# A transformer trunk in fp32: the kernel orders the feed-forward units itself, and six of eight pairs go by seven products

## Chip, cores and metric

One core of a Trainium2 chip runs the whole program. The metric is device time in microseconds of one execution (lower is better), as the median of several runs. Matrix products run on TensorE (PE), elementwise work on VectorE (DVE) and ScalarE (ACT), a little on GpSimd (POOL), and SyncE (SP) issues the loads from device memory.

## The reference

Two layers over 256 tokens of width 2048, all in float32. Each layer is a mixer (attention, recurrence, pooling) and then a gated feed-forward part, each with a residual and a layer norm:

```python
def swiglu(x, w_gate, w_up, w_down):
    return (jax.nn.silu(x @ w_gate) * (x @ w_up)) @ w_down
...
        x = layer_norm(DN_ALPHA * x + y, ln_mix_g[layer], ln_mix_b[layer])
        f = swiglu(x, ffn_w_gate[layer], ffn_w_up[layer], ffn_w_down[layer])
        x = layer_norm(DN_ALPHA * x + f, ln_ffn_g[layer], ln_ffn_b[layer])
```

`w_gate` and `w_up` are 2048 x 5632, `w_down` is 5632 x 2048. The change touches the feed-forward part alone.

## The kernel before

**Products.** Every factor is split into a high and a low part in fp32r: ScalarE casts the high part (`whi`), VectorE subtracts it for the low part (`wlo`; both in `split`, L121 to L123). A product is three matmuls (`mm3`, L285): x low by w high, x high by w high, x high by w low. Each has 128 x 128 stationary values and 512 columns. Weights come as pieces of 128 x 1024 (`load_half`, L145) into `raw` (4 buffers) and `whi`, `wlo` (4 buffers, more where another ring of buffers is open).

**Feed-forward part** (`ffn`, L544). The hidden width is eleven chunks of 512. Chunks 0 and 1 go by `whole` (L548): sixteen pieces, gate and then up, four products of three matmuls each, 192 matmuls a chunk. Their result is gated (ScalarE silu, VectorE multiplication, L568), transposed on PE and split again ("flip"). Chunks 2 to 10 are nine units (`unit`, L448). A unit computes, for two token tiles, gate and up together as 2 x 2 blocks, over eight pairs of 128-deep slices. A pair costs eight products, or seven by a scheme with sums of x (`forms_of`, L404, made once per layer) and sums of w (`load_seven`, L428: VectorE makes `z` and `ze` from a raw tile `rs` of four blocks, and ScalarE and VectorE split them into `sh` and `sl`). `SEVEN` names the pairs that go by seven.

**A unit in time.** First half: for each pair of `SEVEN` four of its seven products, into four banks c11, c12, c22, c21. After the last one the banks are recombined (L472 to L477, one copy, four subtractions, one copy with a sign into c21). Second half: the other three products of those pairs, with a piece of `raw` and the split of `ze` (`zfh`, `zfl`), and the pairs by eight products. Into the first half are laid the eight steps of the down projection of earlier chunks (`down_steps`, L510: one piece, 12 matmuls) and the two flips of the chunk before (8 transposes). With five of eight pairs by seven products a unit has 192 - 15 = 177 matmuls of its own and 96 of the down projection, 273 in all.

**What sets the order.** PE's order in the units is that of the code (`keep_in_program_order` in `mm3`); `ORDER` and `GAPS` place pairs and down steps. For ScalarE, VectorE and SP a scheduler places each instruction by priorities (`tc.high_priority`). `rs`, `sh` and `sl` have two buffers, `z` one.

Of the kernel before, what the change touches and what calls it, by code (L numbers as in the profile page):

```python
# [72 lines left out]
SEVEN = (3, 4, 5, 6, 7)  # L73
GAPS = (1, 1, 1, 0, 2)
ORDER = (3, 0, 4, 5, 1, 6, 7, 2)
# [3 lines left out]
def trunk(ctx: ExitStack, tc: tile.TileContext, a, out):  # L79
# [62 lines left out]
    low = []  # L142
    first = [True]

    def load_half(src, between=()):  # L145
# [5 lines left out]
        with tc.high_priority(offset=400):  # L151
# [5 lines left out]
            for i in range(parts):  # L157
# [7 lines left out]
                with ExitStack() as order:  # L165
                    for ins in behind:
                        order.enter_context(tc.issue_after(ins))
                    low.append(split(hi[:, s, :], lo[:, s, :], raw[:, s, :]))
# [5 lines left out]

    later = []

    def half_done(n=1):
        for entry in list(later):
            entry[0] -= n
            if entry[0] <= 0:  # L180
                later.remove(entry)
                entry[1]()

    def mm_chunk(halves, lhs, outs, tok_major=False, after=None, before=None, seeded=False):
# [36 lines left out]
        else:  # L221
            for i, half in enumerate(halves):
                src = half[0]
                loaded.append(load_half(src, before(i) if before else ()))
                for kks in ((0,), (1,)) if before and i == 0 else ((0, 1),):
                    for tok in range(NT):
                        mms(i, tok, kks=kks)
                half_done()
# [175 lines left out]
    def forms_of(sp, xT, out, seven, tag):  # L404

        n = len(seven)
        xs = sp.tile([P, NT, 2 * n, P], F32, tag="rs", name="xs", bufs=2)
        fs = sp.tile([P, 4, n, P], F32, tag="z", name="fs", bufs=1)
        yield
        for t in range(NT):  # L410
            s = slice(2 * seven[0], 2 * seven[0] + 2 * n)
            nc.vector.tensor_tensor(xs[:, t], xT[0][t][:, s, :].bitcast(F32), xT[1][t][:, s, :].bitcast(F32), op=add)
            yield
        x11, x12, x21, x22 = (xs[:, t, e : 2 * n : 2, :] for t in range(2) for e in range(2))
        e, f, g, h = (fs[:, i] for i in range(4))
        nc.vector.tensor_tensor(e, x22, x21, op=sub)
        nc.vector.tensor_tensor(f, e, x11, op=add)
        yield
        nc.vector.tensor_tensor(g, x11, x21, op=sub)
        nc.vector.tensor_tensor(h, x12, f, op=sub)  # L420
        yield
        hi, lo = split_tile(sp, [P, 4, n, P], fs, tag)
        for i, p in enumerate(seven):
            x = lambda t, k: (xT[0][t][:, k, :], xT[1][t][:, k, :])
            e, f, g, h = (at((hi, lo), slice(None), j, i) for j in range(4))
            out[p] = {"11": x(0, 2 * p), "12": x(0, 2 * p + 1), "22": x(1, 2 * p + 1), "e": e, "f": f, "g": g, "h": h}

    def load_seven(sp, src, room):  # L428

        with tc.high_priority(offset=400):  # L430
            raw = sp.tile([P, 4, NCH], F32, tag="rs", name="rs", bufs=2)
            hi = sp.tile([P, 4, NCH], F32R, tag="sh", name="sh", bufs=2)
            lo = sp.tile([P, 4, NCH], F32R, tag="sl", name="sl", bufs=2)
            z = sp.tile([P, 3, NCH], F32, tag="z", name="z", bufs=1)
            ze = room
            last_load[0] = nc.sync.dma_start(raw, src).ins
            nc.scalar.copy(hi[:, 0], raw[:, 0])
            nc.vector.tensor_tensor(z[:, :2], raw[:, 0:3:2], raw[:, 3:4].to_broadcast([P, 2, NCH]), op=add)
            nc.vector.tensor_tensor(z[:, 2], z[:, 0], raw[:, 2], op=add)  # L439
            nc.vector.tensor_tensor(ze, z[:, 2], raw[:, 1], op=add)  # L440
            nc.vector.tensor_tensor(lo[:, 0], raw[:, 0], hi[:, 0].bitcast(F32), op=sub)
            split(hi[:, 1:], lo[:, 1:], z)
        return lambda i: (hi[:, i, :], lo[:, i, :]), ze


    BEGIN = ((0, "11", "c11"), (3, "f", "c12"), (1, "e", "c22"), (2, "g", "c21"))

    def unit(sp, w, lhs, forms, y, down, flips):  # L448


        def run(n):
            for _ in range(n):
                next(down, None)

        for _ in range(NT):
            run(1)
            flips.pop(0)()
        run(1)
        b = {n: bank("un", 4) for n in ("c11", "c12", "c22", "c21")}
        edge, room = {}, None  # L460
        for i, (p, gap) in enumerate(zip(SEVEN, GAPS)):
            if i % 2:
                room = ap_.tile([P, 4, T], F32R, tag=("y4h", "y4l")[i // 2], name="ze4", bufs=1)
                room = room.rearrange("p (e a) t -> p e (a t)", e=2).bitcast(F32)
            own = room[:, (i + 1) % 2] if i else sp.tile([P, NCH], F32, tag="ze", name="ze", bufs=1)
            wt, edge[p] = load_seven(sp, w[p], own)
            for j, x, name in BEGIN:
                mm3(b[name], forms[p][x], wt(j), i == 0, i == len(SEVEN) - 1, True)
            if i == len(SEVEN) - 1:
                with tc.high_priority(offset=1000):  # L470
# [780 lines left out]
```

## Time and profile before

| what | us |
|---|---|
| median of 3 runs | 2186.62 (2186.35 to 2190.95) |
| the profiled execution, whole | 2190.12 |
| its span, first to last instruction | 2187.8 |
| mean granted TensorE clock | 0.997 |
| DMA over the span | 467.82 MB, 214 GB/s on average |

The profile has a page with shares of the span, a chain of waits followed back from the last instruction, and views of the trace by window, tile and engine. Names such as `wlo<-raw,whi` are the program's tiles, output first. An instruction's shown length is longer than the distance to the next one on a busy engine, since the next begins before the last has drained; distances ("pitches") are what add up.

### The profile page before, as it was taken

To read this page: it belongs to the slowest core of one execution; us is meant where nothing else is said; L and a number is where in the kernel's file an instruction comes from. 1 tells how busy PE (TensorE), PEld (TensorE's weight loads), DVE (VectorE), ACT (ScalarE), POOL (GpSimd) and SP (SyncE) were. 2 spreads that over 40 slices of the span, in tenths; PEclk is the share of its full clock that TensorE was granted. 3 is DMA by queue.
4 is the path that set the end of the run, shared out by engine and by line. 5 is a ranking of instruction groups with operands and counts; after the bars stand their busy time and mean duration, and the time that the engine had idled before them with its cause. 6 is when DMAs were issued, how large, how long until landed. Compare 5 with 4: busy or idle time off the path is not lost.

```text
span 2187.8 us, 27113 instructions
## 1 busy us (share of the span) xinstructions
PE 2148.9 (98%) x9910; PEld 1778.7 (81%) x9910; DVE 1691.1 (77%) x2122; ACT 1215.7 (56%) x1580; POOL 37.5 (2%) x43
## 2 busy tenths in 40 slices
PE   9999999999999999999999999999999999999998
PEld 7888888888878888888888788888788888888876
DVE  6886688676698888888886776675988888888866
ACT  6445534555455566666565554454556666565653
POOL 0000001000000000000000000000000000000000
PEclk9999999999999999999999999999999999999999
DMA  8555545684666776776665663655776766676754
GB/s 293 161 163 182 167 132 189 194 286 143 211 232 241 240 242 238 251 242 220 238 220 194 214 217 121 212 178 174 266 245 239 250 239 219 244 236 244 241 165 172
DMA packets 118613, 467.82 MB, mean 214 GB/s; under 512 B 13904, under 2 KB 16976, under 8 KB 105680
## 3 DMA queue, kind: packets, MB, share of 16 engines
q1 hardware_dynamic: 118480, 466.09, 63.0%
q8 instruction: 78, 1.28, 0.2%
q14 instruction: 55, 0.45, 0.1%
HBM read 463.94 MB, written 2.10 MB: 213 GB/s over the span
## 4 chain that ended last, share of the span: by engine, by line
PE 92%; DVE 3%; ACT 3%; DMA 1%; issue 0%; SPq 0%; ACTq 0%; DVEq 0%
PE acc L288 52%; PE un L288 30%; PE mx L288 6%; PE mx L803 1%; DVE sl L123 1%; PE tr L119 1%; ACT whi L122 1%; ACT sh L122 1%; PE un L119 1%; DVE wlo L123 1%; DMA raw<-in_cd_in 0%; ACT res L541 0%; DVE res L326 0%; DMA raw<-in_ab_in 0%; PE mx L849 0%
## 5 line engine op out<-in xcount | busy, mean ns | idle before, releaser
L123 DVE TENSOR_TENSOR wlo<-raw,whi 128x1024 fp32r<-128x1024 f32 (+1 forms) x671 | 814.7, 1222 | 321.2 <-ACT whi L122 311.8
L122 ACT CAST whi<-raw 128x1024 fp32r<-128x1024 f32 (+1 forms) x671 | 702.6, 1050 | 587.5 <-PE acc L288 302.5
L288 PE MATMUL acc<-whi,yTl 128*128 128x512 f32 x832 | 329.0, 396 | 1.2 <-DVE g L568 1.1
L288 PE MATMUL acc<-whi,yTh 128*128 128x512 f32 x832 | 325.0, 391 | 0.0
L288 PE MATMUL acc<-wlo,yTh 128*128 128x512 f32 x832 | 324.3, 391 | 0.0
L288 PE MATMUL acc<-whi,xTl 128*128 128x512 f32 x800 | 318.4, 398 | 5.2 <-ACT whi L122 5.1
L288 PE MATMUL acc<-whi,xTh 128*128 128x512 f32 x800 | 315.2, 394 | 0.0
L288 PE MATMUL acc<-wlo,xTh 128*128 128x512 f32 x800 | 313.0, 394 | 0.1
L288 PE MATMUL un<-whi,xTh 128*128 128x512 f32 x522 | 203.1, 389 | 0.0
L288 PE MATMUL un<-wlo,xTh 128*128 128x512 f32 x522 | 203.1, 389 | 0.0
L288 PE MATMUL un<-whi,xTl 128*128 128x512 f32 x522 | 203.1, 389 | 0.0
L288 PEld LDWEIGHTS acc<-whi,yTl 128*128 128x128 f32 x832 | 156.6, 188 | 33.6 <-DVE g L568 1.5
L288 PEld LDWEIGHTS acc<-wlo,yTh 128*128 128x128 f32 x832 | 156.6, 188 | 33.3
L288 PEld LDWEIGHTS acc<-whi,yTh 128*128 128x128 f32 x832 | 156.8, 188 | 31.4
L123 DVE TENSOR_TENSOR sl<-z,sh 128x1536 fp32r<-128x1536 f32 x90 | 157.9, 1755 | 29.4 <-ACT sh L122 28.9
L288 PEld LDWEIGHTS acc<-whi,xTl 128*128 128x128 f32 x800 | 151.1, 189 | 35.7 <-ACT whi L122 6.5
L122 ACT CAST sh<-z 128x1536 fp32r<-128x1536 f32 x90 | 133.3, 1481 | 81.3 <-DVE z L439 81.3
L288 PEld LDWEIGHTS acc<-wlo,xTh 128*128 128x128 f32 x800 | 150.9, 189 | 31.5 <-DVE wlo L123 1.2
L288 PEld LDWEIGHTS acc<-whi,xTh 128*128 128x128 f32 x800 | 151.2, 189 | 28.8
L288 PEld LDWEIGHTS un<-whi,xTh 128*128 128x128 f32 x522 | 98.0, 188 | 20.4
L288 PEld LDWEIGHTS un<-whi,xTl 128*128 128x128 f32 x522 | 98.0, 188 | 20.3
L288 PEld LDWEIGHTS un<-wlo,xTh 128*128 128x128 f32 x522 | 98.0, 188 | 20.3
(270 smaller groups left out, 3025.6 us busy)
## 6 DMA issues: line engine op xcount, KB each, us to landing
raw<-in_gu SPq DMA_DIRECT2D x262, 512.0 KB, 4.6
rs<-in_gu SPq DMA_DIRECT2D x90, 1024.0 KB, 6.9
raw<-in_down SPq DMA_DIRECT2D x176, 512.0 KB, 4.3
raw<-in_ab_in SPq DMA_DIRECT2D x127, 512.0 KB, 4.1
raw<-in_cd_in SPq DMA_DIRECT2D x40, 512.0 KB, 4.5
raw<-in_ab_out SPq DMA_DIRECT2D x32, 512.0 KB, 4.6
raw<-in_cd_out SPq DMA_DIRECT2D x32, 512.0 KB, 4.2
bias<-in_na_bias SPq DMA_DIRECT2D x32, 64.0 KB, 4.0
```

The lines of the kernel that those rows point to most:

```text
L119: return nc.tensor.transpose(o, src, eye)
L122: nc.scalar.copy(hi, src)
L123: return nc.vector.tensor_tensor(lo, src, hi.bitcast(F32), op=sub).ins
L288: ins = nc.tensor.matmul(o, lhs[a], rhs[b], start=start and n == 0, stop=stop and n == 2, **more)
L803: nc.tensor.matmul(m[:, 2 * h + s, :], kk[:, h, s * P : (s + 1) * P], qq[:, h, r * P : (r + 1) * P], start=True, stop=True,)
```

## The change

`SEVEN` gains pair 2, so six pairs go by seven products. A unit now has 192 - 18 = 174 matmuls of its own, 270 with the down projection.

The second part is new code. Between chunk 0 and the end of the units nothing is emitted directly any more: a `Plan` records every operation of PE, ScalarE, VectorE and SP with what it reads and writes, and gives each a due time from PE's order, counted back over a table of costs. Then it fills the engines in time, taking of the operations that are ready the one due first, and emits all in that order and pins it on each engine. `SOON` brings the recombination's due times forward by 4 us. PE's order in a unit changes a little: one down step, both flips, one down step, then each of six pairs with a down step behind it; the second half goes by `HALF` ("p" is half a pair by eight products, "s" the rest of a pair by seven). `load_seven` splits in two halves of two blocks, writes one of its sums back into `rs`, and `z` shrinks to two blocks. The forms are made two pairs at a time, inside the plan. Chunk 0 keeps its gate in the tiles y4 instead of the mixer's pool, and that pool closes before chunk 1.

Two places in VectorE's order, with buffer numbers. The first is the border from chunk 0 to chunk 1 of layer 0. `mx` are the up banks of chunk 0; `xs`, `fs`, `rs_4819`, `z_4830` and `f0l` belong to the forms. Before:

```order
L123 TENSOR_TENSOR wlo_4943<-raw_4941,whi_4942 128x1024
L123 TENSOR_TENSOR wlo_4964<-raw_4962,whi_4963 128x1024
L568 TENSOR_TENSOR sil_4610<-sil_4610,mx_4662 128x512
L568 TENSOR_TENSOR sil_4660<-sil_4660,mx_4663 128x512
L123 TENSOR_TENSOR wlo_4993<-raw_4991,whi_4992 128x1024
L123 TENSOR_TENSOR yTl_4665<-tr_4886,yTh_4664 128x4x128
L412 TENSOR_TENSOR xs_4959<-xTh0_3818,xTl0_3820 128x768
```

After (`whi_4840` is the first piece of chunk 1):

```order
L845 TENSOR_TENSOR y4h_4484<-y4h_4484,mx_4663 128x512
L572 TENSOR_TENSOR rs_4819<-xTh0_3818,xTl0_3820 128x512
L572 TENSOR_TENSOR rs_4819<-xTh1_3819,xTl1_3821 128x512
L591 TENSOR_TENSOR z_4830<-rs_4819 128x256
L591 TENSOR_TENSOR z_4830<-z_4830,rs_4819 128x256
L591 TENSOR_TENSOR z_4830<-rs_4819 128x256
L591 TENSOR_TENSOR z_4830<-rs_4819,z_4830 128x256
L572 TENSOR_TENSOR rs_4835<-xTh0_3818,xTl0_3820 128x512
L572 TENSOR_TENSOR rs_4835<-xTh1_3819,xTl1_3821 128x512
L572 TENSOR_TENSOR rs_4842<-xTh0_3818,xTl0_3820 128x512
L535 TENSOR_TENSOR f0l_4844<-z_4830,f0h_4837 128x1024
L535 TENSOR_TENSOR wlo_4848<-raw_4821,whi_4840 128x1024
```

The first `wlo` of chunk 1 was made ahead of chunk 0's gate (`wlo_4943`, say, is one of chunk 1's later gate pieces); now it stands behind the gate's two multiplications (L845, the second is shown) and ten rows of the forms.

The second place is the recombination at the end of a unit's first half (steady unit of layer 0). Before, the last two pairs' rows and the recombination (L473 to L477):

```order
L440 TENSOR_TENSOR ze4_6915<-z_6943,rs_6940 128x512
L123 TENSOR_TENSOR sl_6942<-z_6943,sh_6941 128x1536
L441 TENSOR_TENSOR sl_7304<-rs_7302,sh_7303 128x512
L438 TENSOR_TENSOR z_7305<-rs_7302 128x1024
L473 TENSOR_TENSOR g1_6965<-un_6782,g0_6964 128x512
L439 TENSOR_TENSOR z_7305<-z_7305,rs_7302 128x512
L474 TENSOR_TENSOR un_6782<-g1_6965,un_6783 128x512
L440 TENSOR_TENSOR ze_7301<-z_7305,rs_7302 128x512
L475 TENSOR_TENSOR g1_6965<-g1_6965,un_6784 128x512
L123 TENSOR_TENSOR sl_7304<-z_7305,sh_7303 128x1536
L477 TENSOR_TENSOR un_6783<-g1_6965,un_6783 128x512
```

After (L721 is the recombination; `rs_6473` is a pair of the next unit):

```order
L535 TENSOR_TENSOR sl_6500<-rs_6428,sh_6489 128x1024
L535 TENSOR_TENSOR wlo_6515<-raw_6356,whi_6505 128x1024
L627 TENSOR_TENSOR z_6530<-rs_6473 128x1024
L631 TENSOR_TENSOR rs_6473<-z_6530,rs_6473 128x512
L635 TENSOR_TENSOR ze0_6543<-rs_6473 128x512
L535 TENSOR_TENSOR sl_6549<-z_6530,sh_6541 128x1024
L535 TENSOR_TENSOR sl_6549<-rs_6473,sh_6541 128x1024
L535 TENSOR_TENSOR wlo_6565<-raw_6402,whi_6554 128x1024
L721 TENSOR_TENSOR g1_6575<-un_6342,g0_6563 128x512
L721 TENSOR_TENSOR un_6342<-g1_6575,un_6348 128x512
L721 TENSOR_TENSOR g1_6575<-g1_6575,un_6352 128x512
L721 TENSOR_TENSOR un_6348<-g1_6575,un_6348 128x512
```

The four subtractions stood among the sums and splits of a later pair's weights; now they are side by side, behind a whole pair of the next unit and one piece.

The diff, cut to its core:

```diff
--- before.py
+++ after.py
@@ -70,9 +70,130 @@
-SEVEN = (3, 4, 5, 6, 7)
-GAPS = (1, 1, 1, 0, 2)
-ORDER = (3, 0, 4, 5, 1, 6, 7, 2)
+SEVEN = (2, 3, 4, 5, 6, 7)
+HALF = "psspsspssp"
+SOON = 4000
...
+    COST = {"PE": {512: 227, 128: 90}, "DVE": {1024: 1136, 512: 602, 256: 335}, "ACT": {1024: 960, 512: 530}}
...
+    def op(self, engine, size, fn, reads=(), writes=(), times=1, lag=0, due=0):
+        cost = 50 if engine == "SP" else self.COST[engine][size] * times
+        i = len(self.ops)
+        needs = {}
+        for x in reads:
+            if x in self.wrote:
+                needs[self.wrote[x]] = 1
+            self.read.setdefault(x, []).append(i)
+        for x in writes:
+            if x in self.wrote:
+                needs[self.wrote[x]] = 1
+            for r in self.read.pop(x, ()):
+                needs.setdefault(r, 0)
+            self.wrote[x] = i
+        for place, _ in (*reads, *writes):
+            if isinstance(place, Place) and i not in place.users:
+                place.users.append(i)
+        needs.pop(i, None)
+        first = [p for p, _ in writes if isinstance(p, Place)]
+        self.ops.append((engine, cost, size, fn, needs, first, lag, due))
+        return i
+    def run(self):
+        ops = self.ops
+        n = len(ops)
+        needs = [dict(o[4]) for o in ops]
+        for i, o in enumerate(ops):
+            for p in o[5]:
+                if p.old:
+                    for u in p.old.users:
+                        needs[i].setdefault(u, 0)
+                if p.before:
+                    needs[i].setdefault(p.before.users[0], 0)
+            needs[i].pop(i, None)
+        users = [[] for _ in ops]
+        for i in range(n):
+            for j in needs[i]:
...
+        due, t = [1e12] * n, 0
+        pe = [i for i in range(n) if ops[i][0] == "PE"]
+        for i in pe:
+            due[i], t = t, t + ops[i][1]
+        for i in reversed(order):
+            own = 4500 if ops[i][0] == "SP" else ops[i][1]
+            for j in users[i]:
+                due[i] = min(due[i], due[j] - own - (ops[i][6] + 130 if ops[j][0] != ops[i][0] else 0))
+        due = [d - o[7] for d, o in zip(due, ops)]
+        ready, left = [0.0] * n, [len(x) for x in needs]
+        free = dict.fromkeys(("PE", "ACT", "DVE", "SP"), 0.0)
+        open_ = {e: {i for i in range(n) if ops[i][0] == e and not left[i]} for e in free}
+        queue, at, start, bus = 0, 0.0, [0.0] * n, 0.0
+        for _ in range(n):
+            best = None
+            for e in free:
+                if e == "PE":
+                    picks = [pe[queue]] if queue < len(pe) and not left[pe[queue]] else []
+                else:
+                    picks = open_[e]
+                if picks:
+                    t = max(free[e], min(ready[i] for i in picks))
+                    c = min((t, due[i], i) for i in picks if ready[i] <= t)
+                    best = c if best is None else min(best, c)
+            t, _, i = best
+            e, cost, _, _, _, _, lag, _ = ops[i]
+            open_[e].discard(i)
+            queue += e == "PE"
+            start[i], free[e] = t, t + cost
+            end = t + cost
+            if e == "SP":
+                bus = max(t + 1600, bus) + ops[i][2] / 360 * 1000
+                end = bus + 300
+            for j in users[i]:
+                x = end if needs[j][i] else t + cost
+                ready[j] = max(ready[j], x + (130 + lag * needs[j][i] if ops[j][0] != e else 0))
+                left[j] -= 1
+                if not left[j]:
+                    open_[ops[j][0]].add(j)
+        seen = set()
+        for i in sorted(range(n), key=lambda i: (start[i], i)):
+            with self.tc.high_priority(offset=400):
+                for ins in ops[i][3]():
+                    if ops[i][0] in seen:
+                        self.tc.keep_in_program_order(ins)
+                    seen.add(ops[i][0])
...
+        def parts(hi, lo, src, size, high, low, reads, at=0):
+            plan.op("ACT", size, lambda: [nc.scalar.copy(high(), src())], reads, [(hi, at)])
+            plan.op(
+                "DVE",
+                size,
+                lambda: [nc.vector.tensor_tensor(low(), src(), high().bitcast(F32), op=sub)],
+                [*reads, (hi, at)],
+                [(lo, at)],
+            )
...
+        def load_seven(src, i):
+            raw = tile_of(sp, [P, 4, NCH], "rs", 2)
+            z = tile_of(sp, [P, 2, NCH], "z", 1)
+            hi, lo = (tile_of(sp, [P, 4, NCH], n, 2, F32R) for n in ("sh", "sl"))
+            ze = edge_place(i)
+            load(raw, src, 1049)
+            r, g = raw.get, z.get
+            tt = nc.vector.tensor_tensor
+            plan.op(
+                "DVE",
+                1024,
+                lambda: [tt(g(), r()[:, 0:3:2], r()[:, 3:4].to_broadcast([P, 2, NCH]), op=add)],
+                [(raw, 0)],
+                [(z, 0)],
+            )
+            plan.op("DVE", 512, lambda: [tt(r()[:, 2], g()[:, 0], r()[:, 2], op=add)], [(z, 0), (raw, 0)], [(raw, 1)])
+            for n, src, reads in ((0, lambda: r()[:, 0:3:2], [(raw, 0), (raw, 1)]), (1, g, [(z, 0)])):
+                h, l = ((lambda x=x, n=n: x.get()[:, 2 * n : 2 * n + 2]) for x in (hi, lo))
+                parts(hi, lo, src, 1024, h, l, reads, n)
+            plan.op("DVE", 512, lambda: [tt(ze.get(), r()[:, 2], r()[:, 1], op=add)], [(raw, 0), (raw, 1)], [(ze, 0)])
+            return lambda j: ((hi, j // 2), (lo, j // 2), lambda: (hi.get()[:, j], lo.get()[:, j])), ze
...
+            run = lambda: next(down, None)
+            run()
+            for _ in range(NT):
+                flip()
+            run()
+            b = {n: of_bank("un") for n in ("c11", "c12", "c22", "c21")}
+            edge = {}
+            for i, p in enumerate(SEVEN):
+                wt, edge[p] = load_seven(w[p], i)
+                for j, x, name in BEGIN:
+                    v, more = forms[p][x]
...
+            plain = [(p, n) for p in range(8) if p not in SEVEN for n in range(2)]
+            seven = list(SEVEN)
+            for kind in HALF:
+                if kind == "s":
+                    p = seven.pop(0)
+                    wt = piece(w[p][:, 1:3])
+                    more("c11", forms[p]["12"], wt(0))
+                    more("c12", forms[p]["h"], wt(1))
+                    hi, lo = (tile_of(sp, [P, NCH], n, 2, F32R) for n in ("zfh", "zfl"))
+                    parts(hi, lo, edge[p].get, 512, hi.get, lo.get, [(edge[p], 0)])
+                    more("c21", forms[p]["22"], ((hi, 0), (lo, 0), lambda hi=hi, lo=lo: (hi.get(), lo.get())))
+                    continue
+                p, n = plain.pop(0)
+                wt = piece(w[p][:, 2 * n : 2 * n + 2])
+                ks = (2 * p + n, 2 * p + 1 - n)
+                for tok in range(NT):
+                    for kk in range(2):
+                        more(f"c{tok + 1}{n + 1}", (lhs(tok, ks[kk]), ()), wt(kk))
...
+        for n in range(len(SEVEN) // 2):
+            make_forms(n, SEVEN[2 * n : 2 * n + 2])
+        ys = {0: new_y()}
+        for tok in range(NT):
+            z = edge_place(1 + tok)
+            flips.append((z.get, (z, 0), ys[0], tok))
+        y = new_y()
+        whole(1, y)
+        ys[1] = y
+        for units, chunks in ROUNDS:
+            down = down_steps(chunks, [ys[c] for c in chunks], chunks[0] == 0)
+            for c in units:
+                ys[c] = new_y()
+                unit(w[c], ys[c], down)
+            assert next(down, None) is None
+        plan.run()
+        groups = [ys[c].get() for c in LAST]
+        return groups, [lambda g=g, y=y, t=t: transpose4(g(), *(e[:, :, t * P : (t + 1) * P] for e in y.get()), 1000) for g, _, y, t in flips]
 
     def ffn(layer, xT, res, mix_pool, close_mix, keep, last):
...
+        y4 = fourth()
+        sil = y4[0].rearrange("p (e a) t -> p e (a t)", e=2).bitcast(F32)
+        gouts = [acc() for _ in range(NT)]
+        def silu(tok):
+            nc.scalar.activation(sil[:, tok], gouts[tok], AF.Silu)
+        mm_chunk([(w[0, i][:, :2], (2 * i, 2 * i + 1)) for i in range(8)], lhs, gouts, tok_major=True, after=silu)
+        uouts = [mxp() for _ in range(NT)]
+        def gated(tok):
+            with tc.high_priority(offset=1000):
+                nc.vector.tensor_tensor(sil[:, tok], sil[:, tok], uouts[tok], op=mult)
+        mm_chunk([(w[0, i][:, 2:], (2 * i + 1, 2 * i)) for i in range(8)], lhs, uouts, after=gated)
+        close_mix()
         stack = ExitStack()
...
+        groups, flips = inner(layer, later_pool(stack, f"sp{layer}"), xT, y4, res)
```

More of the change, by code (lines that the diff above doesn't have):

```diff
@@ L140, in trunk @@
     last_load = [None]
-    low = []
     first = [True]
@@ L167, in load_half @@
                         order.enter_context(tc.issue_after(ins))
-                    low.append(split(hi[:, s, :], lo[:, s, :], raw[:, s, :]))
+                    split(hi[:, s, :], lo[:, s, :], raw[:, s, :])
         return hi, lo
@@ L401, in out_proj @@
         return xT
[L404 to L443, printed above, removed]
@@ new lines, in whole @@
+                        product(gate[tok], lhs(tok, 2 * i + kk), wt(kk), (i, kk) == (0, 0), (i, kk) == (7, 1))
+                if i == 3:
+                    for _ in range(NT):
+                        flip()
+            for i in range(8):
+                wt = piece(w[c, i][:, 2:])
+                if not i:
+                    up = [of_bank("un") for _ in range(NT)]
+                for tok in range(NT):
+                    for kk in range(2):
+                        product(up[tok], lhs(tok, 2 * i + 1 - kk), wt(kk), (i, kk) == (0, 0), (i, kk) == (7, 1))
@@ new lines, in inner @@
+        for n in range(len(SEVEN) // 2):
+            make_forms(n, SEVEN[2 * n : 2 * n + 2])
+        ys = {0: new_y()}
+        for tok in range(NT):
+            z = edge_place(1 + tok)
[9 more added lines that the diff above has]
+            assert next(down, None) is None
@@ L579, in ffn @@
-        stack = ExitStack()
-        forms, making, sps, flips = {}, [], [], []
-        def make():
-            with tc.issue_after(low[-1]):
-                for _ in range(2):
-                    if next(making[0], "end") == "end":
-                        making.pop(0)
-                        if not making:
-                            return
-            later.append([1, make])
-        def change_rooms():
-            close_mix()
-            sps.append(later_pool(stack, f"sp{layer}"))
-            making.append(forms_of(sps[0], xT, forms, SEVEN[:3], "fm"))
-            making.append(forms_of(sps[0], xT, forms, SEVEN[3:], "fn"))
-            later.append([1, make])
@@ L598, in ffn @@
-        groups = {c: None for c in range(2)}
-        groups[0] = whole(0, True)
-        later.append([6, change_rooms])
-        groups[1] = whole(1, False)
+        y4 = fourth()
[4 more added lines that the diff above has]
+        mm_chunk([(w[0, i][:, :2], (2 * i, 2 * i + 1)) for i in range(8)], lhs, gouts, tok_major=True, after=silu)
@@ L602, in ffn @@
+        uouts = [mxp() for _ in range(NT)]
[4 more added lines that the diff above has]
+        close_mix()
+        stack = ExitStack()
         open_banks("units")
+        groups, flips = inner(layer, later_pool(stack, f"sp{layer}"), xT, y4, res)
         wd = a[f"down{layer}"]
-        for units, chunks in ROUNDS:
-            down = down_steps(wd, chunks, [groups[c] for c in chunks], res, chunks[0] == 0)
-            for c in units:
-                groups[c] = new_yT()
-                unit(sps[0], w[c], lhs, forms, groups[c], down, flips)
@@ L618, in ffn @@
         seed, evac, _ = residual_tools(res, None, None, stats)
-        yl = y_lhs([groups[c] for c in LAST])
+        yl = y_lhs(groups)
         def some(ns, order):
```

328 lines of the change are left out of this document (215 added, 113 removed).

## The prediction

> **What bounds the kernel now.** I read the page's shares first, then its chain of waits, then the windows of one period, then the instructions inside it. The page:
> ```profile
> PE 2148.9 (98%) x9910; PEld 1778.7 (81%) x9910; DVE 1691.1 (77%) x2122; ACT 1215.7 (56%) x1580; POOL 37.5 (2%) x43
> ...
> PE 92%; DVE 3%; ACT 3%; DMA 1%; issue 0%; SPq 0%; ACTq 0%; DVEq 0%
> ...
> L288 PE MATMUL un<-whi,xTh 128*128 128x512 f32 x522 | 203.1, 389 | 0.0
> ```
> TensorE carries the chain, so a matmul that goes is worth its spacing in time, and the rest is small waits. A busy PE hides some of these, since one matmul is shown 0.389 us long although they follow each other more closely. So I count work against period. The chain in order of time, over the units of the first layer and then the second, repeats one piece:
> ```profile
> 643.93 26.52 PE un L288 x117
> ...
> 771.71 26.52 PE un L288 x117
> ...
> 1091.19 26.52 PE un L288 x117
> ...
> 1593.23 26.52 PE un L288 x117
> ```
> That piece is the second half of a unit (the products behind the recombination). 117 matmuls in 26.52 us are **0.2267 us each**. Seven periods from 643.93 to 1091.19 are **63.89 us each**. The window of one of them, and, of the waits in it, the one that PE itself has:
> ```profile
> 771.71:835.57 63.86, 63.13 (x282) 51.94 (x282) 53.88 (x58) 38.51 (x47) 0.00 (x0) 1.00 0.70 239
> ```
> ```profile
> PE un L288 <- DVE sl L123: 0.7, 1, 0.7
> ```
> The columns are stretch, length, then busy time and count of PE, weight load, VectorE, ScalarE and GpSimd, granted clock, DMA share, GB/s. VectorE is idle for 10.0 us of the period. The chain inside it:
> ```profile
> 800.95 0.43 PE un L119 x4
> ...
> 820.95 2.51 PE acc L288 x11
> ...
> 825.02 1.39 ACT sh L122
> ...
> 826.44 1.77 DVE sl L123
> 828.21 0.04 issue
> 828.25 1.88 PE un L288 x7
> ```
> The code issues 273 matmuls and 8 transposes (two groups of four, 0.43 each, the first row) per unit: 273 x 0.2267 + 0.86 = 62.75. So a unit **waits 1.14 us**. The other rows show where: at the last pair by seven products, whose low half (sl) comes late from VectorE.
>
> Two stretches lie outside the steady units: from the start of the second hidden chunk to the second half of the first unit.
> ```profile
> 557.62 10.88 PE acc L288 x48
> ...
> 602.10 2.72 PE acc L288 x12
> ...
> 1508.70 10.88 PE acc L288 x48
> ```
> They last 643.93 - 557.62 = 86.31 and 1593.23 - 1508.70 = 84.53 us. Their work is 192 + 156 matmuls and 16 transposes: 348 x 0.2267 + 1.72 = 80.61. They wait **5.7 and 3.9 us**.
>
> **The change, part by part.**
>
> *Fewer matmuls.* One more pair of eight goes by 21 matmuls instead of 24: 3 per unit, 54 over 18 units, 54 x 0.2267 = **-12.2 us**, all on the path. [...]
>
> *More work beside it.* Pitches (start to start) of VectorE and ScalarE come from neighbours in the timeline:
> ```profile
> 583.07 0.42 DVE L416 TENSOR_TENSOR fs<-xs 128x256 f32<-128x256 f32 x1
> 583.40 0.42 DVE L419 TENSOR_TENSOR fs<-xs 128x256 f32<-128x256 f32 x1
> ...
> 783.28 1.22 DVE L438 TENSOR_TENSOR z<-rs 128x1024 f32<-128x1024 f32 x1
> 784.41 0.68 DVE L123 TENSOR_TENSOR zfl<-ze,zfh 128x512 fp32r<-128x512 f32 x1
> 785.01 1.22 DVE L123 TENSOR_TENSOR wlo<-raw,whi 128x1024 fp32r<-128x1024 f32 x1
> ```
> ```profile
> 771.76 1.05 ACT L122 CAST whi<-raw 128x1024 fp32r<-128x1024 f32 x1
> 772.70 0.60 ACT L524 ACTIVATE acc<-res 128x512 f32<-128x512 f32 x1
> ```
> So 1024 columns are 1.13 us on VectorE and 0.94 on ScalarE, 512 are 0.60, 256 are 0.33. The new pair loses two low halves (2.26) and gains z, two sl, one wlo (4.52) and three operations of 512 (1.80): +4.1 us of VectorE per unit, 53.9 to 57.9 in a period that can be 62.1. ScalarE gains three casts of 1024 and one of 512 for two: about +1.5 on 38.5. The load grows by half a megabyte, some 3%. I cost all this at nothing; idle time of both engines covers it. Without that cover it would be 4.1 x 18 = 74 us, so it matters whether VectorE's idle time falls where it is needed. That is the next term.
>
> *The order in the units.* A wait of 1.14 us in 16 steady units (18.2) and 9.6 in the two outer stretches, 27.8 in all, can go: bounds 0 and -27.8. Let X be the moment PE ends the first pair of a unit. It then alternates down-projection halves and pairs (5.44 for both), and needs the recombined bank c21 at X + 5 x 5.44 + 2.72 + 1.36 = X + 31.3. VectorE cannot split pair 3 before X, for only two sh/sl buffers exist; with the cast (0.94) and hand-offs it starts at X + 1.3. The order shows 30 rows from there through the third L721 (the second listing of the section on the change has their end): 19 of 1024 and 11 of 512, 19 x 1.13 + 11 x 0.60 = 28.1. That ends at X + 29.4, and ScalarE's copy into c21 (0.6 and two hand-offs of 0.13) at X + 30.3: **1.0 us to spare**. By the same count VectorE has done all earlier rows some 4 us before X + 1.3 and waits for that buffer, so it has no debt from earlier. What can use up the 1.0 us is the load of rs. Its two buffers force each load to wait until VectorE has read the one two pairs before (on SP's queue it stands behind a raw load that was freed earlier); until it is needed VectorE has seven rows, 5 x 1.13 + 2 x 0.60 = 6.85 us. Landing in the window above:
> ```profile
> L436 SPq DMA_DIRECT2D rs<-in_gu x5: 328/328/328, 779.4 to 832.4; - x5
> ...
> DMA to landing us min/median/max: 4.9/7.2/8.0
> ```
> With 0.25 for the hand-offs (an estimate), 7.2 makes VectorE wait 0.6 us. This happens at every second load (one wait delays the next release too), twice per unit: 1.2, and PE waits 0.2. At 4.9 PE waits 0, at 8.0 it waits 2 x 1.4 - 1.0 = 1.8. I take 0.3, by the median and a little for the other hand-offs: 18 x 0.3 = **+5.4**, ends 0 and +32. [...]
>
> *The border into the planned part.* Here the new order adds a wait. On VectorE both multiplications of the first chunk wait for PE's last products, and behind them now stand ten rows of the forms before the first wlo of the second chunk (first listing); before, that wlo stood far ahead, and PE had no gap at 557.62 and 1508.70. On ScalarE the first whi stands behind the cast of the forms. PE can do two matmuls without wlo (0.45 us). From PE's last matmul: hand-off 0.2 (0.389 shown less 0.227, and 0.04 issue), second multiplication 0.60, five adds of 512 (3.0), four of 256 (1.32), f0l and wlo (2.26), hand-off 0.13, less 0.45: 7.06. ScalarE's part is shorter: its whi is done some 5.6 after PE's last matmul. **+7.1 per layer, +14.2.** Bounds: 0, if it were covered, which nothing in the order does; 8.5 each, if the forms' strided reads cost a little more.
>
> *At nothing:* the first chunk's gate in y4; the earlier end of the mixer's pools; four whi/wlo buffers instead of more in the second chunk (four pieces take PE 10.9 us, and one round of landing, cast and subtract some 7); the flips side by side, with 4.5 us before a bank is wanted again. The end of a layer keeps its order; I take 0, ends -1 and +3 each.
>
> **Sum.** Span 2187.8 - 12.2 - 27.8 + 5.4 + 14.2 = 2167.4, or -20.4. The profiled execution took 2190.12 (2.3 more than its span) and lies 3.5 above the median of 2186.62. From the median: **2166.2 us**, 0.9% faster.
>
> **Rivals.**
>
> *The waits stay.* The static order may put its lateness elsewhere, and a unit waits 1.14 as now: 18 x 1.14 = 20.5 instead of 5.4, so 2181. For it: only 1.0 us to spare. Against: the one wait of now has a cause (sl late) that the second listing moves away.
>
> *Slower: loads of rs.* Each us of landing over 7.2 is met twice per unit, 36 us in all. Without any wait the sum is 2160.8; 25.8 us more are 1.43 per unit, reached at a landing of 7.8 us; at 8.3 it is 2.4 per unit, 2204. For it: 8.0 occurs now, and a unit moves 3% more in 3% less time. Against: the median is 7.2 at 239 GB/s, and in the new order no other load starts within 3 us ahead of the critical ones.
>
> *No gap at the border:* 2152. It would take VectorE to pass over waiting rows; nothing in the trace shows that.
>
> **How the numbers follow.** Forecast (2157 to 2174): 60%. Waits stay (2175 to 2186): 18%. Slow loads (2183 to 2210): 12%. No gap (2146 to 2156): 5%. Anything else: 5%. The range 2152 to 2188 leaves out the worse part of the slow loads, some of the third and the rest, under 2 in 10. Within 0.2% of before is 2182.3 to 2191.0, about what a measurement of this kernel can tell from no change. Faster: 60 + 5 + two thirds of 18 + 2 = 79%; same 10%; slower 11%.
>
> **What would show it.** Periods of the 26.5 us piece's successor (102 matmuls) near 62.4; 54 matmuls fewer; at each border a PE gap of some 7 us that ends on wlo; VectorE about 92% busy in a unit; if PE waits in a unit, on the copy into c21. I am wrong if the periods stay above 63, if rs lands later than 7.8, or if the border shows no gap.

## The result, and the profile after

The changed kernel takes **2175.28 us** (median of 4 runs, 2172.67 to 2177.14) against 2187.31 us for the kernel before in the same job: ratio **0.9941**, 95% interval [0.9924, 0.9958]. That is 12.0 us or 0.6% less, where 20.4 us or 0.9% were forecast: the right sign, 60% of the size, inside the range of 2152 to 2188 but just above the band of 2157 to 2174 that had the 60% chance. In the profiled executions the span falls from 2187.8 to 2173.0, by 14.8 us, and the rest of this section is about those 14.8.

The page of the changed kernel, its shares and its chain:
```profile
PE 2136.8 (98%) x9856; PEld 1772.6 (82%) x9856; DVE 1768.5 (81%) x2226; ACT 1239.2 (57%) x1618; POOL 37.4 (2%) x43
...
PE 92%; DVE 4%; DMA 2%; issue 1%; ACT 1%; SPq 0%; DVEq 0%; ACTq 0%
```
9856 is 54 matmuls fewer than before, as it should be. Next, what PE waited for (total, times, longest):
```profile
PE acc L557 <- ACT whi L531: 11.5, 2, 5.7
...
PE acc L557 <- DVE wlo L535: 1.5, 2, 0.8
PE un L557 <- ACT un L731: 1.1, 3, 0.7
```
Before, the longest of this list was:
```profile
PE un L288 <- DVE sl L123: 14.0, 18, 1.2
```
These 14.0 us on sl are gone. Two long waits have come, one per layer, at the border to chunk 1, and a few small ones on the copy into c21. The second halves of the units (102 matmuls now) in the chain, in order of time; the rows of the second layer from 1719.35 are its second to seventh unit:
```profile
963.76 23.28 PE un L557 x102
1026.02 23.37 PE un L557 x102
1719.35 23.39 PE un L557 x102
...
2031.22 23.27 PE un L557 x102
```
The last five periods, 1719.35 to 2031.22, are 62.37 us each, against work of 270 x 0.2267 + 0.86 = 62.07. So a steady unit still waits 0.3 us, where it waited 1.14.

Now a ledger for each layer's planned stretch, from the end of the last product of chunk 0 to the end of the last product of the last unit. Its ends in PE's timeline of before (a row starting chunk 1, a row ending the last unit, for each layer):
```profile
557.46 0.39 PE L288 MATMUL acc<-whi,xTl 128*128 128x512 f32 x1
...
1181.22 0.39 PE L288 MATMUL un<-wlo,xTh 128*128 128x512 f32 x1
...
1508.54 0.39 PE L288 MATMUL acc<-whi,xTl 128*128 128x512 f32 x1
...
2130.45 0.39 PE L288 MATMUL un<-wlo,xTh 128*128 128x512 f32 x1
```
And of the changed kernel (last product of chunk 0, last product of the last unit):
```profile
556.88 0.39 PE L398 MATMUL mx<-wlo,xTh 128*128 128x512 f32 x1
...
1173.38 0.40 PE L557 MATMUL un<-wlo,xTh 128*128 128x512 f32 x1
...
1500.81 0.39 PE L398 MATMUL mx<-wlo,xTh 128*128 128x512 f32 x1
...
2116.19 0.40 PE L557 MATMUL un<-wlo,xTh 128*128 128x512 f32 x1
```
A product that ends a stretch holds PE for 0.2267 more. Before, the two stretches last 623.99 and 622.14; after, 616.50 and 615.38. Their work is 192 matmuls of chunk 1, nine units and ten groups of transposes at 0.86: 2649 x 0.2267 + 8.6 = 609.1 before, 2622 x 0.2267 + 8.6 = 603.0 after. So PE lost 14.9 and 13.0 us before (27.9, the forecast's 27.8), and loses 13.5 and 12.4 now (25.9). The change took most of the waits out of the units and put nearly as much back in another place: **of the 14.2 us gained in the stretches 12.2 are the matmuls, 2.0 the order.**

Where the 25.9 are, at the border of the first layer, by windows (stretch, length, busy PE, weight load, VectorE, ScalarE, GpSimd, **granted clock**, DMA share, GB/s):
```profile
550.00:556.80 6.80, 6.80 (x32) 5.63 (x31) 0.69 (x1) 0.00 (x0) 0.00 (x0) 1.00 0.00 0
556.80:563.00 6.20, 0.48 (x4) 0.06 (x2) 5.55 (x11) 2.05 (x3) 0.00 (x0) 0.75 0.00 1
563.00:570.20 7.20, 6.42 (x15) 4.60 (x15) 6.68 (x9) 3.74 (x5) 0.00 (x0) 0.51 0.53 173
570.20:577.00 6.80, 6.80 (x31) 5.63 (x30) 5.99 (x8) 3.15 (x4) 0.00 (x0) 1.00 0.99 358
```
In the first row VectorE, ScalarE and the DMA engines stand idle although chunk 1's work is near; in the second PE waits while VectorE makes forms; in the third, PE is at work again and its granted clock is 0.51. The matmuls there, in PE's timeline:
```profile
564.99 0.80 PE L557 MATMUL acc<-wlo,xTh 128*128 128x512 f32 x1 [0.78 <-DVE wlo L535]
565.59 0.63 PE L557 MATMUL acc<-whi,xTl 128*128 128x512 f32 x1
566.01 0.63 PE L557 MATMUL acc<-whi,xTh 128*128 128x512 f32 x1
```
They follow each other by 0.43 us instead of 0.2267. Chunk 1's third matmul starts at 564.99 where 557.56 was possible, 7.4 us late; the slow ones that follow add 2.5 in this layer and 1.6 in the second (its wait is 7.4 too). Ledger of both layers:

| term | forecast | profiled execution |
|---|---|---|
| 54 matmuls | -12.2 | -12.2 |
| waits of before that go | -27.8 | -27.9 |
| border: wait | +14.2 | +14.8 |
| border: matmuls at the lower clock behind it | none | +4.1 |
| waits left in 18 units | +5.4 | +7.0 |
| outside the stretches | 0 | -0.6 |
| sum | -20.4 | -14.8 |

### The profile page after: what moved, and what is told of

The parts are those of the page before. It is cut to its first block, busy times and chain, and to the rows that moved or that the text cites. A ratio compares the mean times of both kernels' runs of the same rounds, so it can differ in the third digit from the quotient of the medians.

```text
span 2173.0 us, 27222 instructions
## 1 busy us (share of the span) xinstructions
PE 2136.8 (98%) x9856; PEld 1772.6 (82%) x9856; DVE 1768.5 (81%) x2226; ACT 1239.2 (57%) x1618; POOL 37.4 (2%) x43
## 3 DMA queue, kind: packets, MB, share of 16 engines
q1 hardware_dynamic: 118480, 475.53, 63.6%
q8 instruction: 77, 1.26, 0.2%
## 4 chain that ended last, share of the span: by engine, by line
PE 92%; DVE 4%; DMA 2%; issue 1%; ACT 1%; SPq 0%; DVEq 0%; ACTq 0%
PE un L557 33%; PE acc L398 32%; PE acc L557 19%; PE mx L398 4%; PE mx L1047 1%; PE tr L240 1%; PE un L240 1%; DMA raw<-in_down 1%; DVE wlo L244 1%; DMA rs<-in_gu 1%; DVE wlo L535 1%; ACT whi L243 0%; DMA raw<-in_cd_in 0%; PE mx L1093 0%; PE mx L1308 0%
## 5 line engine op out<-in xcount | busy, mean ns | idle before, releaser
L531 ACT CAST whi<-raw 128x1024 fp32r<-128x1024 f32 x356 | 372.2, 1050 | 211.8 <-PE acc L557 98.5
L244 DVE TENSOR_TENSOR wlo<-raw,whi 128x1024 fp32r<-128x1024 f32 (+1 forms) x297 | 360.7, 1224 | 154.9 <-ACT whi L243 152.4
L535 DVE TENSOR_TENSOR wlo<-raw,whi 128x1024 fp32r<-128x1024 f32 x356 | 430.5, 1220 | 66.4 <-ACT whi L531 62.5
L243 ACT CAST whi<-raw 128x1024 fp32r<-128x1024 f32 (+1 forms) x297 | 309.4, 1049 | 300.6 <-PE acc L398 186.7
L557 PE MATMUL acc<-whi,yTl 128*128 128x512 f32 x576 | 225.8, 392 | 0.0
L531 ACT CAST sh<-z 128x1024 fp32r<-128x1024 f32 x108 | 113.8, 1053 | 126.7 <-DVE z L627 73.2
L535 DVE TENSOR_TENSOR sl<-rs,sh 128x1024 fp32r<-128x1024 f32 x108 | 131.7, 1219 | 26.2 <-ACT sh L531 26.2
L531 ACT CAST sh<-rs 128x1024 fp32r<-128x1024 f32 x108 | 113.3, 1049 | 42.2 <-PE un L557 27.7
L627 DVE TENSOR_TENSOR z<-rs 128x1024 f32<-128x1024 f32 x108 | 131.7, 1220 | 1.8 <-DMA rs<-in_gu 1.0
L535 DVE TENSOR_TENSOR sl<-z,sh 128x1024 fp32r<-128x1024 f32 x108 | 131.6, 1218 | 0.0
```

Source lines behind the costliest of these rows:

```text
L243: nc.scalar.copy(hi, src)
L244: return nc.vector.tensor_tensor(lo, src, hi.bitcast(F32), op=sub).ins
L531: plan.op("ACT", size, lambda: [nc.scalar.copy(high(), src())], reads, [(hi, at)])
L535: lambda: [nc.vector.tensor_tensor(low(), src(), high().bitcast(F32), op=sub)],
L557: yield nc.tensor.matmul(o.get(), x[i], r[j], start=begin and n == 0, stop=end and n == 2, **kw)
L627: lambda: [tt(g(), r()[:, 0:3:2], r()[:, 3:4].to_broadcast([P, 2, NCH]), op=add)],
```

## The experiments

All are compared with runs of the kernel before on the same chip. A ratio r is turned into us as r x 2185.

### Forms behind the first pieces

The plan starts its clock with empty load buffers and a free VectorE, so at its time 0 the forms are all that VectorE can do. In truth four raws are long in at that moment: in the changed kernel they are issued from 534.2 to 540.9 and land 4.0 to 5.4 us later, over 10 us before PE ends chunk 0 at 557.1. The edit tells it so:
```
-        free = dict.fromkeys(("PE", "ACT", "DVE", "SP"), 0.0)
+        free = {"PE": 0.0, "ACT": 0.0, "DVE": 1300.0, "SP": 0.0}
+        early = 4
...
+            if e == "SP" and early:
+                early, end = early - 1, t
-            if e == "SP":
+            elif e == "SP":
```
VectorE's order now has four wlo of chunk 1 ahead of chunk 0's gate products, and the forms come one by one between later pieces.

> Same work; only the plan's clock at its start is changed (first four raws are in, VectorE free at 1.3 us), so that four wlo of chunk 1 stand ahead of the forms. The border costs 10.1 us a layer in the changed kernel by its trace: 7.7 us until the first piece is ready, then ten to twelve matmuls at twice the distance. Theory (the border is the whole shortfall): about 20 us less than the changed kernel, near 2155 us, ratio to before 0.985. Rival (the forms only take their 11 us of VectorE from a later place, and PE waits there, in chunk 1 or at the first form of the first unit): under 8 us less, 2168 or more.

Measured: **2156.8 us**, ratio 0.9859 [0.9846, 0.9873]. PE at the border of the first layer (the end of chunk 0, then chunk 1):
```profile
557.01 0.39 PE L401 MATMUL mx<-wlo,xTh 128*128 128x512 f32 x1
557.24 0.39 PE L560 MATMUL acc<-whi,xTl 128*128 128x512 f32 x1
```
No gap. The stretches take 606.4 and 608.1, so 3.4 and 5.1 us of waits are left of 13.5 and 12.4: 17.4 us less in the two stretches of the trace, 18.5 in the medians. The rival, that the forms' 11 us of VectorE must be paid elsewhere, falls. This version beats both kernels: 1.4% below before, where the change as made gives 0.6%.

### Was the lower clock a cost of its own?

20 matmuls per layer into a bank that nobody reads were put into the border's wait of the changed kernel:
```
+            fill = of_bank("un")
+            r = xT[0][1][:, 0:4, :].rearrange("p k t -> p (k t)")
+            def filler():
+                for _ in range(20):
+                    yield nc.tensor.matmul(fill.get(), xT[0][0][:, 0, :], r, start=True, stop=True)
+            plan.op("PE", NCH, filler, [], [(fill, 0)], 0)
```

> The changed kernel with 20 matmuls more per layer at the border between chunk 0 and chunk 1, into a bank that nobody reads, in time in which PE waits anyway. Theory (the ten to twelve matmuls at 0.43 us behind the wait are slow because PE stood still for 6 us and its clock was lowered): granted clock 1.00 behind the border, 2.2 to 2.9 us less per layer, about 2170 us. Rival (they are slow because their operands come one by one, or by the phase of the program): same slow matmuls, 2175 us or a little more.

Measured: 2175.73 us, ratio 0.9950 [0.9936, 0.9964], no less than the changed kernel, as the rival had it. The windows say more (the first two rows of the first layer, from chunk 1's first matmul on, the others of the second, through the wait and behind it):
```profile
563.30:570.30 7.00, 5.72 (x24) 4.41 (x25) 6.71 (x9) 2.82 (x3) 0.00 (x0) 1.00 0.47 147
570.30:577.00 6.70, 6.70 (x35) 5.64 (x34) 4.98 (x7) 4.98 (x6) 0.00 (x0) 1.00 0.97 360
...
1499.70:1504.50 4.80, 3.61 (x16) 2.64 (x15) 4.73 (x10) 2.03 (x3) 0.00 (x0) 1.00 0.00 0
1504.50:1511.50 7.00, 5.74 (x17) 4.36 (x18) 6.69 (x9) 3.88 (x5) 0.00 (x0) 0.76 0.54 135
```
In the first layer the clock stayed at 1.00 and no matmul was slow, although the pieces came one by one at the same pace: the lower clock that the changed kernel has there (0.51) comes from PE's standstill, not from the operands. The stretch is 1.3 us shorter there. In the second layer two rests (1.2 us behind the filler, 1.2 us before the first wlo) were enough to lower it again for eight matmuls; the first layer had the same two rests (1.2 and 1.3 us) and no slow matmul, so rests of this length decide nothing by themselves. And in this run the copy into c21 was late 5 times, 3.8 us in all against 1.1, which took back what the first layer gained. So the cause, PE's long standstill, is shown in one layer by clock and spacing; its price is too small for the time to show it here.

### The order alone: the scheduler's order of the same operations

Operations are emitted as they are written, and only PE's order is pinned:
```
-        for i in sorted(range(n), key=lambda i: (start[i], i)):
-            with self.tc.high_priority(offset=400):
+        for i in range(n):
+            with self.tc.high_priority(offset=0 if ops[i][0] == "PE" else 400):
...
-                    if ops[i][0] in seen:
+                    if ops[i][0] in seen and ops[i][0] == "PE":
```

> Same operations, six pairs and the same order on PE; on ScalarE, VectorE and SP the scheduler orders them again (from the order in which they are written), not the plan. Its VectorE has four wlo of chunk 1 ahead of the forms, so no border wait (20 us less). Theory (the plan's order is what removed the waits inside the units): 1.1 us or more a unit come back, 16 to 18 units, so 2155 + 18 to 2155 + 30, about 2175 to 2185 us, with PE waiting on sl or on the copy into c21 in every unit. Rival (the waits went because the operations were cut up differently, 512 columns less behind sl, and the order matters little): near 2157 us, level with the kernel whose forms stand later.

Measured: **2238.88 us**, ratio 1.0238 [1.0219, 1.0258], 82 us above the kernel whose forms stand later and far over what either theory gave. What PE waited for, and VectorE's timeline ahead of one such wait:
```profile
PE un L557 <- ACT un L731: 53.5, 16, 5.3
```
```profile
916.15 0.68 DVE L721 TENSOR_TENSOR g<-un,g 128x512 f32<-128x512 f32 x1
916.75 1.21 DVE L627 TENSOR_TENSOR z<-rs 128x1024 f32<-128x1024 f32 x1
917.89 0.68 DVE L721 TENSOR_TENSOR un<-g,un 128x512 f32<-128x512 f32 x1
918.48 0.68 DVE L631 TENSOR_TENSOR rs<-z,rs 128x512 f32<-128x512 f32 x1
919.09 1.22 DVE L535 TENSOR_TENSOR wlo<-raw,whi 128x1024 fp32r<-128x1024 f32 x1
920.22 0.68 DVE L721 TENSOR_TENSOR g<-g,un 128x512 f32<-128x512 f32 x1
```
The scheduler takes the subtractions (L721) by turns with whatever is ready, so the third, on which c21 hangs, ends 4.7 us after the first began. By the spans of the traces (2243.1 and 2156.2) the two kernels are 86.9 us apart. Of this, 53.5 are these waits; most of the rest is the clock: behind waits of 3 to 5 us, 163 matmuls of the two stretches stand 0.38 to 0.5 us apart instead of 0.2267 (the granted clock is 0.50 from 921.50 to 925.00, say), 32.5 us by that difference. I had not counted this in either expectation.

The rival of this run is answered only in part. The order matters a great deal for the copy into c21. But no wait on sl is left here either, so it is not shown that the plan's order is what removed the 14.0 us of them: the new cutting of the rows or PE's new order may have done it, or the time that the longer waits on c21 give VectorE.

### Rows between the subtractions, nothing else

The kernel with later forms, and one rule more in its plan:
```
-                    c = min((t, due[i], i) for i in picks if ready[i] <= t)
+                    c = min((t, due[i] + 1e6 * (e == "DVE" and ops[i][7] and after), i) for i in picks if ready[i] <= t)
...
+            if e == "DVE":
+                after = ops[i][7]
```

> The kernel whose forms stand later (2156.8 us), with one rule more in the plan: after one subtraction of the c21 chain VectorE takes another row if one is ready. So z (1.22 us) and rs (0.69 us) of the next piece stand between the first three subtractions in 16 units; all other orders are the same. Theory (what the plan's order brings is that the chain into c21 stands in one piece): c21 is 1.9 us later, less up to 1 us to spare, so 16 to 30 us more, 2173 to 2187 us, and 16 waits on the copy into c21. Rival (late landings of rs make those waits, not the rows' order): 2157 to 2162 us.

Measured: 2174.75 us, ratio 0.9950 [0.9938, 0.9962], 20 us more than with the chain in one piece.
```profile
PE un L563 <- ACT un L737: 20.5, 16, 1.3
```
Sixteen waits of 1.28 us, and no slow matmul behind them. For comparison, the chain in one piece in VectorE's timeline of the kernel with later forms:
```profile
1014.36 0.68 DVE L724 TENSOR_TENSOR g<-un,g 128x512 f32<-128x512 f32 x1
1015.15 0.70 DVE L724 TENSOR_TENSOR un<-g,un 128x512 f32<-128x512 f32 x1
1015.95 0.69 DVE L724 TENSOR_TENSOR g<-g,un 128x512 f32<-128x512 f32 x1
1016.67 0.70 DVE L724 TENSOR_TENSOR un<-g,un 128x512 f32<-128x512 f32 x1
```
From the start of the first to the end of the third it takes 2.3 us; with the two rows between it takes 3.6 (768.17 to 771.79, say), and the rows quoted for the scheduler's order take 4.7. The rival falls: late landings are not needed to explain these waits, two foreign rows are enough. The chain became 1.3 us longer and PE waited 1.3 us, so there was nothing to spare in front of c21. The 4 us head start that the plan gives the chain's due times (SOON) is not what keeps it together: with SOON at 0 every engine's order comes out the same.

### What the sixth pair is worth

Five pairs with the plan. In a first form each unit ran one step too few of the second projection, so that run left out one of sixteen steps in each of eight rounds (96 matmuls):
```
-SEVEN = (2, 3, 4, 5, 6, 7)
-HALF = "psspsspssp"
+SEVEN = (3, 4, 5, 6, 7)
+HALF = "pspspspspsp"
...
-        for n in range(len(SEVEN) // 2):
+        for n in range((len(SEVEN) + 1) // 2):
```

> Five pairs by seven products as before, with the plan. Theory (the sixth pair is worth its 54 matmuls, 54 x 0.2267 = 12.2 us, and the VectorE work that it adds costs nothing): 2187.5 us, level with the kernel before; the distance of two steady units 63.0 us. Rival (the added VectorE work, 4 us a unit, causes what waits are left, 0.3 to 0.4 us a unit and the late landings): 12.2 less 5, about 2182 us, distance 62.75.

Measured: 2196.97 us, ratio 1.0042 [1.0029, 1.0056], though it leaves out 21.8 us of matmuls:
```profile
PE un L557 <- ACT un L731: 25.4, 16, 2.3
```
The step that fell away is the 2.7 us of matmuls between the last pair and the first use of c21. Without this cover the copy is 1.6 us late in each of 16 units. As a test of the sixth pair it says nothing. The second form runs that step behind the last pair:
```
+                    run()
                 run()
```

> Five pairs by seven products with the plan, and all steps of the second projection (the run e2_five_pairs dropped one of sixteen in each of eight rounds, 96 matmuls). 54 matmuls more than the changed kernel, border as in it. Theory (the sixth pair is worth its 54 matmuls and its VectorE work costs nothing): 2175.3 + 12.2 = 2187.5 us, no c21 waits. Rival (the sixth pair's VectorE work, 4 us a unit, costs something): 2180 to 2184 us. Second rival (as in e2, where PE waited 1.6 us a unit on the copy into c21): 2200 us or more.

Measured: 2184.22 us, ratio 0.9996 [0.9988, 1.0005]: **the plan with five pairs is level with the kernel before** (2184.62 in the same job), and 0.55% or 12 us above the changed kernel, which is the 12.2 us of the matmuls. The second halves of its units in the second layer:
```profile
1660.13 26.52 PE un L557 x117
...
2036.87 26.52 PE un L557 x117
```
Six periods of 62.79 on work of 62.75: no waits in these units at all. So the order gains some 20 us in the units, and the border, which is as long in this kernel (11.5 us on whi), gives them back. Six pairs leave 0.3 us a unit, so the sixth pair's VectorE work costs about 5 us at most, less than this comparison of medians can resolve.

### More VectorE work

Each ze is computed twice, in the kernel with later forms (the plan.op of L635 stands there twice).

> The kernel whose forms stand later (2156.8 us), with each ze computed twice: six 512-column rows more per unit, 6 x 0.69 = 4.1 us, so VectorE would be busy 62.0 of some 62.3 us of a unit. Theory (VectorE work inside a unit costs nothing as long as it fits, as the prediction took for the 4.1 us that the sixth pair adds): at most 5 us more, 2157 to 2162 us. Rival (at that load every row stands behind another and the chain into c21 or a wlo comes late): 10 us more or worse, from 2167 us.

Measured: 2176.16 us, ratio 0.9957 [0.9946, 0.9969], **21 us more**; the rival was right. What PE waited for in the units, and the window of one period:
```profile
PE un L560 <- DVE sl L538: 8.0, 16, 2.4
...
PE un L560 <- DVE yTl L660: 3.9, 8, 0.5
```
```profile
1839.84:1903.44 63.60, 62.86 (x280) 51.28 (x279) 61.62 (x69) 40.79 (x50) 0.00 (x0) 1.00 0.69 250
```
The period grew from 62.3 to 63.6 us, with VectorE at 61.6 of it. Over the six periods from 1649.2 to 2029.6 VectorE is idle 1.9 us a period: 0.8 ahead of rows that wait for the load of rs, 0.6 in hand-overs from one row to the next that needs it, most of the rest behind casts. So VectorE was all but full, with little room to make up for a load that came late. At 57.9 us busy of 62.3 the changed kernel stands close to this edge.

### c21 later

```
-HALF = "psspsspssp"
+HALF = "ppsspsspss"
...
-            plain = [(p, n) for p in range(8) if p not in SEVEN for n in range(2)]
+            plain = [(p, n) for n in range(2) for p in range(8) if p not in SEVEN]
+            later = []
...
+                late = [(f"c2{n + 1}", lhs(1, ks[kk]), wt(kk)) for kk in range(2)]
...
+                if n == 0:
+                    later += late
+                for name, x, r in later if len(plain) < 3 and n == 0 else late if n else ():
+                    more(name, (x, ()), r)
```

> The kernel whose forms stand later (2156.8 us), with PE's order in the second half of a unit changed: the four products of the plain pairs that go into c11 stand first, then the four into c21, so c21 is needed 1.36 us later. Theory (what is left of waits in the units is the copy into c21, 2.5 us in all): those waits vanish, 2154 us. Rival (the next rows are late then: whi and wlo of the second piece, or silu of the gate): 2157 us or more.

Measured: 2161.67 us, ratio 0.9893 [0.9881, 0.9906], 7 us more by the ratios (3.4 by the spans of the traces), with no wait on c21 left:
```profile
PE un L243 <- DVE g L671: 6.2, 6, 1.7
PE tr L243 <- DVE g L671: 5.4, 2, 3.4
```
The half now ends on two pairs by seven products, and the gate products are late for the flips of the next unit (the first row) and for those at the end of a layer (the second); in the kernel with later forms these two rows are 0.4 and 2.3 us. The rival was right: the wait moved.

## Why the prediction was right, and where it was off

**Fewer matmuls, -12.2: right**, by the count of the page and by the five-pair kernel (12 us); the matmuls stand 0.2267 us apart in the units before and after.

**The waits in the units, -27.8 with +5.4 left: the size came out, the reason did not.** Periods are 62.37, forecast 62.4. Where PE still waits in a steady unit it is for the copy into c21, as forecast. The units lose 7.0 in all, 0.39 each instead of 0.3. But the 0.3 was derived from loads of rs that come late and use up 1.0 us to spare, and the trace shows neither. VectorE was idle 1.8 us in all ahead of the 108 rows that first read rs, where 1.2 us in every unit were forecast:
```profile
L627 DVE TENSOR_TENSOR z<-rs 128x1024 f32<-128x1024 f32 x108 | 131.7, 1220 | 1.8 <-DMA rs<-in_gu 1.0
```
And there was nothing to spare. In a steady unit, the first split that the count starts from, the copy into c21, and PE's first matmul into that bank:
```profile
1752.72 1.23 DVE L535 TENSOR_TENSOR sl<-rs,sh 128x1024 fp32r<-128x1024 f32 x1 [1.50 <-ACT sh L531]
...
1782.30 0.60 ACT L731 ACTIVATE un<-g 128x512 f32<-128x512 f32 x1 [0.66 <-DVE g L721]
...
1782.95 0.50 PE L557 MATMUL un<-whi,xTl 128*128 128x512 f32 x1
```
X is 1751.66 here, so PE needs the bank at X + 31.3, as counted. But the 30 rows end at 1782.27 and take 29.55 us, where the count has 28.1, and the copy ends 0.05 us before PE's matmul. The count gives every row its spacing among independent rows (0.60 for 512 columns); a row that needs the one just before it starts 0.72 to 0.80 us behind it where that one has 512 columns, and 1.25 to 1.26 instead of 1.13 where it has 1024, and nine of the 30 stand behind such a hand-over. So two errors of about 1 us a unit, late loads that did not come and hand-overs that were not counted, cancelled: that the size came out is luck.

The landing of rs was put too late: 7.2 us by the rows of before; after the change:
```profile
L541 SPq DMA_DIRECT2D rs<-in_gu x6: 328/328/328, 969.8 to 1023.3; - x6
...
DMA to landing us min/median/max: 4.7/4.8/7.0
```
With the loads apart in time the median is 4.8. Over all loads of rs, those that SP issues at least 4.8 us behind the load before them land in 4.6 to 5.2 us (30 after the change, 16 before it); those issued less than 2.9 us behind it have a median of 6.9 after (46) and 7.05 before (58); in between both occur. That other loads near by made the 7.2 is my reading of it; no run tried that alone. The 0.25 for the hand-offs was an estimate: where VectorE does wait for rs, at 880.42, z starts 0.10 us after the landing, and SP issues the next load, at 880.01, 0.03 after the last read of its buffer.

**The border, +14.2: the failing step was the size of this term**, "+7.1 per layer, +14.2". The wait itself came as derived, 14.8. What the derivation left out is what a standstill does to PE afterwards: 4.1 us of matmuls at a granted clock of 0.51 in the first layer (563.00 to 570.20) and 0.50 in the second (1507.50 to 1512.10). The trace of before showed it, and I read past it. Its windows around the wait in the first unit (same columns):
```profile
612.00:616.00 4.00, 2.41 (x10) 1.38 (x9) 4.00 (x6) 0.36 (x1) 0.00 (x0) 1.00 0.57 199
616.00:620.00 4.00, 4.00 (x12) 3.14 (x11) 2.89 (x3) 1.99 (x2) 0.00 (x0) 0.57 0.91 240
```
Two waits within 4 us (1.0 and 0.9), and the next 8 matmuls cost 1.6 us more than they should. I had put this into "wait 5.7 us" of that stretch. These rows show matmuls that slow down behind pauses; PE's longest pause inside that trace is 2.9 us (from 1236.24), so no row of it prices one of 6. After the change the pauses ahead of chunk 1's first and third matmul are 5.9 and 1.2 us in each layer, and the 4.1 us stand behind them. The forms' strided reads, the condition of the bound of 8.5, cost no more than counted: their rows of 512 columns stand 0.60 apart (three from 560.78 to 562.58), those of 256 stand 0.33 to 0.46.

**VectorE's added 4.1 us, at nothing: right for this kernel, with no room behind it.** The same amount once more cost 21 us. That VectorE is idle for 4 us of a unit was not the safety that the prediction took it for.

**The base.** Of the 9 us between forecast and median, 5.6 are the terms above (span 2167.4 forecast, 2173.0 measured). The rest is that the profiled execution of before lay about 3 us above its median and that of after at its median, which no step of the sum could know.

**The rivals.** "The waits stay" gave 2181 and lay nearer to 2175 than the forecast did, for the wrong reason: the waits went. "Slow loads" did not come: rs lands sooner, not later (a median of 4.9 us over all its loads, 6.9 before). "No gap at the border" gave 2152, and the kernel with later forms, which has none, takes 2157.

## What to carry to other kernels

A planner that starts with an empty machine plans its first microseconds wrong: tell it what is already loaded and which engine is still busy, or its first rows land in front of the work that is due. Price a wait by its length and by what follows it, since slow matmuls can stand behind a wait on TensorE: here 2.5 and 1.6 us behind waits of 7.4. Count a row that needs the row before it at its own, longer distance (here 0.72 to 0.80 us instead of 0.60). And an order is worth what its longest chain is worth: here four subtractions in one piece or by turns with other rows made 20 us, and an engine that is idle 7% of a period had no room for 7% more work.

## What the runs showed of the hardware

- The lower clock makes the spacing 0.427 us where the steady rows have 0.2267, and the granted clock of such a stretch reads 0.50 (after the change, 565.60 to 569.80) to 0.57 (where the window takes in a few other matmuls).
- What lowers it is not the length of one pause alone (pauses here are start to start, less 0.2267). In the scheduler's order twelve pauses of 3.11 us are alike: behind eleven of them 5 to 13 matmuls are slow, behind one (989.11) none. In the run with more VectorE work a pause of 2.31 us did nothing and one of 2.57 us was followed by eight slow matmuls. Two pauses close together lowered it before the change (1.0 and 0.9 us, the windows above) and in the filler's second layer (1.4 and 1.4), and did not in the filler's first (1.4 and 1.4). Sixteen pauses of 1.44 us, alone in their unit (the rows between the subtractions), never did. What decides between them no run here shows.
- Dependent rows on VectorE start 0.72 to 0.80 us after one another (the four subtractions above) where independent ones of the same 512 columns start 0.60 apart (in the scheduler's order, 916.15 and 916.75). Taking turns fills the 0.1 to 0.2 us between them and costs a whole foreign row each time.
